# Finishing the down product of a decoder block tile by tile, with three steps held back instead of two

## The chip, the core and the metric

The kernel runs on one core of a Trainium2 chip. A core has a matrix engine (TensorE, "PE" in the profile, its weight loads "PEld"), a vector engine (VectorE, "DVE"), a scalar engine for activation functions (ScalarE, "ACT"), GpSimd ("POOL") and an engine that mostly issues transfers (SyncE, "SP"). Each engine works through its own queue of instructions in order and waits on semaphores that others raise. Sixteen DMA engines move data between the on-chip memory and DRAM; a transfer is started from the queue of SyncE or of ScalarE. The metric is the time of one execution on the device in microseconds (us), lower is better.

## The reference

The kernel computes one decoder block on 1024 tokens with 1024 channels in float32: a mixer (pooling and windowed attention, merged by gates, and an output projection), a residual with a norm, and then a feed-forward part, again with a residual and a norm. What the change touches are the norms and the last lines:

```python
def _rmsnorm(x, g):
    xf = x.astype(jnp.float32)
    r = lax.rsqrt(jnp.mean(xf * xf, axis=-1, keepdims=True) + EPS)
    return (xf * r * g.astype(jnp.float32)).astype(x.dtype)
...
    mix = jnp.einsum('bsd,de->bse', merged, w_out[l])
    x = x + _rmsnorm(mix, g_mix_post[l])

    h2 = _rmsnorm(x, g_mlp_pre[l])
    ff = jnp.einsum('bsf,fd->bsd',
                    jnp.square(jax.nn.relu(jnp.einsum('bsd,df->bsf', h2, w_up[l]))), w_down[l])
    x = x + _rmsnorm(ff, g_mlp_post[l])
```

So every token row of `ff` (1024 values) is squared and averaged, the root of that mean plus EPS is inverted, the row is scaled by it and by a gain, and the residual x1 is added.

## The kernel before, in words

**Precision and products.** Float32 matmuls are made of three passes: each operand is split into a high part and a low remainder (`split`, L97: a cast on ScalarE at L98 and a subtraction on VectorE at L99), and high x high, high x low and low x high are summed (`PASSES`, L32). The large products are done by a Strassen-like scheme: seven half-size products instead of eight, summed into the quarters of the result.

**The down product** (L945 to L1085) is the last stage. The token rows fall into 8 tiles of 128 (0 to 3 the upper half, 4 to 7 the lower), the channels into two halves of 512 (`dj` 0 and 1). The seven products run in the order `PRODUCTS = (1, 5, 2, 3, 6, 7, 4)`. Each has `NS = 8` steps over the 4096 hidden channels; a step is 24 matmuls (2 blocks x 4 tiles x 3 passes) into four banks of the accumulator memory, one a tile. The operands of a step are made two steps ahead (`AHEAD = 2`, `operands`, L975): a load of f (`raw`, four buffers), a weight block that is resident (24 buffers) or streamed, a difference of weights where the scheme wants one (L1004 for product 4), and two splits. The split parts of f have six buffers, so three steps' worth.

**Its end.** In product 4 the steps before the last `LATE = 2` go step by step over all four tiles; the last two are held back and then run tile by tile (L1078), so that tile 4 is complete first, then 5, 6 and 7. For each of them the bank is added to `u` (L1079, VectorE); `fin_half` squares it with a running sum on ScalarE (L1021) and multiplies by the gain in place on VectorE (L1022); then `finish` does the rest for tiles 4 and 5 together, then for 6, then for 7: add the two halves' sums (L1026), the reciprocal root in `rsqrt` (L101: root on ScalarE at L104, then small steps on VectorE at L106 to L116, a reciprocal with one Newton step), load x1 into a staging buffer (L1030), and for both halves one fused multiply and add and a store (L1033, L1034). The lower half's other channels (`v`) have had their square and gain after product 7 (L1073), and the upper half is finished after product 6 (L1084).

**The output projection** (L706 to L754) has the same norm in `mean_sq`: two squares with sums, an addition on VectorE (L710), `rsqrt`. `out_post` uses it on the projection, `out_norm` on the new residual rows, once each for 8 tiles. Transposes of the normed rows (L761) then feed the up product.

**Order.** A planner in the tile layer sets the order of the instructions on each engine out of the program and its own estimate of durations, allocates buffers and places the semaphores; the program's order is its priority. So the written order is not quite that on the engines.

Of the kernel before, what the change touches and what calls it, by code (L numbers as in the profile page):

```python
# [50 lines left out]
def block_kernel(ctx: ExitStack, tc, xt, x, consts, vecs, sinks, b_qkv, g_post, g_mlp, g_mlp_post,  # L51
                 w_qkv, w_u, w_g, w_pool, w_bp, w_ba, w_o, w_up, w_dn, x1_dram, spill, f_dram, out):
    nc = tc.nc
    act, dve, pool, pe = nc.scalar, nc.vector, nc.gpsimd, nc.tensor
# [27 lines left out]
    def at(tag, bufs, shape, dt=F32):  # L82
        return ap_.tile([P] + shape, dt, tag=tag, name=nm(tag), bufs=bufs)

    def bank(tag, shape=None):
        return ps.tile([P] + (shape or [512]), F32, tag=tag, name=nm(tag))

    def small(n=8, tag="sm"):
        return sp.tile([P, n], F32, tag=tag, name=nm(tag))

    def flat(t):
        return t.rearrange("p a b -> p (a b)")
# [8 lines left out]
    def rsqrt(out_r, sums, n):  # L101

        s = small()
        act.activation(s[:, :n], sums, AF.Sqrt, scale=1.0 / D, bias=eps)  # L104
        ms = small()
        dve.tensor_scalar(ms[:, :n], sums, 1.0 / D, EPS, ALU.mult, ALU.add)  # L106
        r = small()
        dve.reciprocal(r[:, :n], s[:, :n])
        t = small()
        if n == 1:  # L110
            dve.scalar_tensor_tensor(t[:, :1], r[:, :1], r[:, :1], ms[:, :1], ALU.mult, ALU.mult)
        else:
            dve.tensor_tensor(t[:, :n], r[:, :n], r[:, :n], ALU.mult)
            dve.tensor_tensor(t[:, :n], t[:, :n], ms[:, :n], ALU.mult)
        dve.tensor_scalar(t[:, :n], t[:, :n], -0.5, 1.5, ALU.mult, ALU.add)
        dve.tensor_tensor(out_r, r[:, :n], t[:, :n], ALU.mult)  # L116
# [83 lines left out]
    for n in range(NT):  # L200
        pe.matmul(bss[:, n:n + 1], sq[:, n * P:(n + 1) * P], ones, start=n == 0, stop=n == NT - 1)
    rsqrt(r1, bss[:, :NT], NT)


# [423 lines left out]
    for p in range(8):  # L628
# [4 lines left out]
        tag = "at" if p % 2 == 0 else "mm"  # L633
# [72 lines left out]
    def mean_sq(src_halves, junk_halves):  # L706
        a = small(2, "sq")
        for i in range(2):
            act.activation(junk_halves[i], src_halves[i], AF.Square, accum_out=a[:, i:i + 1])
        dve.tensor_tensor(a[:, 0:1], a[:, 0:1], a[:, 1:2], ALU.add)  # L710
        r = small(1, "rr")
        rsqrt(r, a[:, 0:1], 1)
        return r

    def halves(t):
# [148 lines left out]
    gfin_b = bcast(g_mlp_post, D)  # L864
# [54 lines left out]
    for p in range(1, NP):  # L919
# [3 lines left out]
        tag = "at" if p % 2 == 0 else "mm"  # L923
# [27 lines left out]
    rp = rpool.__enter__()  # L951
    dl = ctx.enter_context(tc.tile_pool(name="dl", bufs=16, reuse_waits="tile"))

    def acc4(name):
        return [dl.tile([P, 512], F32, tag="acc", name=nm(name), bufs=16) for _ in range(4)]
# [4 lines left out]
    sq = sp.tile([P, 2, NT], F32, tag="fsq", name="fsq", bufs=1)  # L960
    rr = sp.tile([P, NT], F32, tag="frr", name="frr", bufs=1)
    junk = dl.tile([P, 512], F32, tag="junk", name="junk", bufs=1)
    res = {}

    def resident(name, s_):
        t = rp.tile([P, 2, 512], F32, tag="w", name=nm(name))
# [8 lines left out]
    def operands(i, s_):  # L975

        if i == 1 and s_ in early_raw:
            ft, wt = early_raw[s_]
            resident("B11", s_)
        else:  # L980
            if i == 1:
                resident("B11", s_)
            ft = raw_tile()
            nc.sync.dma_start(ft, f_block(A_OF[i], s_))
            if i == 1:
                wt = res["B11", s_]
            elif i == 5:
                resident("B12", s_)
                wt = res["B11", s_]
                dve.tensor_tensor(wt, res["B12", s_], wt, ALU.subtract)  # L990
            elif i == 2:
                wt = streamed("B21", s_)
            elif i == 3:
                resident("B22", s_)
                wt = res["B22", s_]
            elif i == 6:
                wt = res["B11", s_]
                dve.tensor_tensor(wt, res["B22", s_], wt, ALU.subtract)
            elif i == 7:
                wt = res["B12", s_]  # L1000
                dve.tensor_tensor(wt, res["B22", s_], wt, ALU.subtract)
            else:
                wt = streamed("B21", s_)
                dve.tensor_tensor(wt, wt, res["B11", s_], ALU.subtract)  # L1004
        fo = wslot([2, 512]), wslot([2, 512])
        split(*fo, ft)
        wo_ = ar([2, 512]), ar([2, 512])
        split(*wo_, wt)
        opers[i, s_] = fo, wo_

    def down_mm(i, s_, bs, after, order):
        for s2, k2, t in order:
            fo, wo_ = opers[i, s2]
            for j, (fh, wh) in enumerate(PASSES):
                pe.matmul(bs[t], fo[fh][:, k2, t * P:(t + 1) * P], wo_[wh][:, k2, :],  # L1015
                          start=not after and s2 == 0 and k2 == 0 and j == 0,
                          stop=s2 == NS - 1 and k2 == 1 and j == 2, skip_group_check=after)

    def fin_half(n, dj, v):

        act.activation(junk, v, AF.Square, accum_out=sq[:, dj, n:n + 1])  # L1021
        dve.tensor_tensor(v, v, gfin_b[:, dj * 512:(dj + 1) * 512], ALU.mult)  # L1022

    def finish(n0, n1, hv):
        ns = slice(n0, n1)
        dve.tensor_tensor(sq[:, 0, ns], sq[:, 0, ns], sq[:, 1, ns], ALU.add)  # L1026
        rsqrt(rr[:, ns], sq[:, 0, ns], n1 - n0)
        for n in range(n0, n1):
            xs = stage([D])
            nc.sync.dma_start(xs, x1_dram[n])  # L1030
            for dj in range(2):
                o = xs[:, dj * 512:(dj + 1) * 512]
                dve.scalar_tensor_tensor(o, hv[dj][n % 4], rr[:, n:n + 1], o, ALU.mult, ALU.add)  # L1033
                nc.sync.dma_start(out[n][:, dj * 512:(dj + 1) * 512], o)  # L1034

    PRODUCTS = (1, 5, 2, 3, 6, 7, 4)
    LATE = 2
    steps = [(i, s_) for i in PRODUCTS for s_ in range(NS)]
    u, v, c11, c12 = acc4("u"), acc4("v"), acc4("c11"), acc4("c12")
    banks = {}  # L1040
# [4 lines left out]
    for j, (i, s_) in enumerate(steps):  # L1045
        if j + AHEAD < len(steps):
            operands(*steps[j + AHEAD])
        if s_ == 0 and i not in (2, 3):
            tag = "mm" if i in (5, 7) else "at"
            banks[i] = [bank(tag) for _ in range(4)]  # L1050
        bs = banks[{2: 1, 3: 5}.get(i, i)]
        if i != 4 or s_ < NS - LATE:
            down_mm(i, s_, bs, i in (2, 3), [(s_, k2, t) for k2 in range(2) for t in range(4)])
            if s_ < NS - 1:
                continue
        elif s_ < NS - 1:
            continue
        for t in range(4):
            if i == 1:
                act.copy(u[t], bs[t])  # L1060
            elif i == 5:
                act.copy(v[t], bs[t])
            elif i == 2:
                act.copy(c11[t], bs[t])
                fin_half(t, 0, c11[t])
            elif i == 3:
                act.copy(c12[t], bs[t])
            elif i == 6:
                dve.tensor_tensor(u[t], u[t], bs[t], ALU.add)
                dve.tensor_tensor(c12[t], c12[t], u[t], ALU.add)  # L1070
                dve.tensor_tensor(v[t], v[t], u[t], ALU.add)
                fin_half(t, 1, c12[t])
            elif i == 7:  # L1073
                dve.tensor_tensor(v[t], v[t], bs[t], ALU.add)
                dve.tensor_tensor(u[t], u[t], bs[t], ALU.add)
                fin_half(4 + t, 1, v[t])
            else:
                down_mm(i, s_, bs, False, [(s2, k2, t) for s2 in range(NS - LATE, NS) for k2 in range(2)])  # L1078
                dve.tensor_tensor(u[t], u[t], bs[t], ALU.add)  # L1079
                fin_half(4 + t, 0, u[t])  # L1080
                for n0, n1 in ((), ((4, 6),), ((6, 7),), ((7, 8),))[t]:
                    finish(n0, n1, (u, v))
        if i == 6:
            finish(0, 4, (c11, c12))  # L1084
    rpool.__exit__(None, None, None)  # L1085


# [68 lines left out]
```

## Time and profile before

| | us |
|---|---|
| median of 3 runs | 1163.75 (1163.31 to 1164.55) |
| the profiled execution | 1163.43 |
| its span, first to last instruction | 1161.6 |
| TensorE busy | 1137.1 |
| VectorE busy | 827.4 |
| ScalarE busy | 533.8 |
| granted TensorE clock | 0.996 |

In rows in order of time the columns are the start and the duration in us, the engine, the line of the program, the operation, the tile written and the tile read with their shapes, the count, and in brackets how long the engine had been idle before and what ended that. The chain of work is followed back from the last instruction to what released each one. Rows of waits give the engine that waited, what it waited for, the total in us, the number of times and the longest. Buffer numbers are left out of names: `at` and `mm` are accumulator banks, `u`, `v`, `c` sums of products, `fsq` the sums of squares, `sm` small tiles, `frr` the factors, `raw` loaded blocks, `wh` and `ar` their split parts.

### The profile page before, as it was taken

The page shows a single profiled execution, that of the slowest core. Times are in us where ns is not written, and L with a number is a line of the kernel's source. Part 1 is how long each engine was busy: PE and PEld are TensorE (multiplying, and loading weights), DVE is VectorE, ACT ScalarE, POOL GpSimd, SP SyncE. Part 2 cuts the span into 40 slices and gives each one's busy share as a digit, 9 for nine tenths or more (in the row PEclk, how much of TensorE's full clock was granted, in tenths as well). Part 3 has the DMA queues.
Part 4 walks back from the last instruction along what each step waited for, and adds up shares of the span by engine and source line. Part 5 has one row for each costly group of instructions (what it writes and reads, how often), then busy time and mean ns, then how long its engine had stood idle before and what let it go on. Part 6 is the DMA issues. An engine that isn't in the chain of part 4 may idle for free.

```text
span 1161.6 us, 14370 instructions
## 1 busy us (share of the span) xinstructions
PE 1137.1 (98%) x5356; PEld 941.3 (81%) x5356; DVE 827.4 (71%) x1337; ACT 533.8 (46%) x926; POOL 53.5 (5%) x66
## 2 busy tenths in 40 slices
PE   7999999999999999999999999999999999999995
PEld 6888888788888887888788888888888888888884
DVE  7767899888754585777998766667558945447795
ACT  6445655653332233464655453535344345344341
POOL 3411100000000050000000000000000000000000
PEclk9999999999999999999999999999999999999998
DMA  7202114545245453333266434353788564332852
GB/s 257 66 1 91 38 55 163 200 172 172 110 174 189 145 199 109 127 128 127 91 217 217 171 128 181 118 181 118 285 294 295 202 194 133 91 104 77 273 181 91
DMA packets 66167, 179.11 MB, mean 154 GB/s; under 512 B 6192, under 2 KB 6192, under 8 KB 66096
## 3 DMA queue, kind: packets, MB, share of 16 engines
q1 hardware_dynamic: 60480, 157.99, 40.3%
q10 hardware_dynamic: 5616, 20.19, 4.5%
q8 instruction: 42, 0.69, 0.3%
q14 instruction: 29, 0.24, 0.1%
HBM read 127.82 MB, written 50.33 MB: 153 GB/s over the span
## 4 chain that ended last, share of the span: by engine, by line
PE 91%; DVE 4%; ACT 2%; DMA 2%; issue 1%; SPq 0%; DVEq 0%; ACTq 0%
PE mm L408 21%; PE at L408 16%; PE at L1015 15%; PE mm L1015 11%; PE mm L345 8%; PE mm L732 5%; PE mm L347 4%; PE mm L147 3%; PE at L307 2%; PE at L268 2%; PE mm L153 1%; PE at L147 1%; PE at L300 1%; DMA st<-in_w_up_dram 1%; DVE T L99 1%
## 5 line engine op out<-in xcount | busy, mean ns | idle before, releaser
L1015 PE MATMUL at<-ar,wh 128*128 128x512 f32 x744 | 169.3, 389 | 0.0
L1015 PEld LDWEIGHTS at<-ar,wh 128*128 128x128 f32 x744 | 139.6, 188 | 29.0
L1015 PE MATMUL mm<-ar,wh 128*128 128x512 f32 x576 | 131.0, 389 | 0.0
L99 DVE TENSOR_TENSOR wh<-raw,wh 128x1024 fp32r<-128x1024 f32 x53 | 64.8, 1224 | 86.4 <-ACT wh L98 86.4
L1015 PEld LDWEIGHTS mm<-ar,wh 128*128 128x128 f32 x576 | 108.1, 188 | 22.5
L98 ACT CAST wh<-st 128x512 fp32r<-128x512 f32 (+1 forms) x106 | 67.0, 641 | 119.6 <-PE mm L408 36.9
L98 ACT CAST wh<-raw 128x1024 fp32r<-128x1024 f32 x53 | 55.8, 1053 | 134.5 <-PE at L1015 63.4
L99 DVE TENSOR_TENSOR wh<-st,wh 128x512 fp32r<-128x512 f32 (+1 forms) x106 | 82.9, 790 | 18.3 <-ACT wh L98 16.1
L408 PE MATMUL mm<-gr,wh 128*128 128x512 f32 x300 | 72.4, 391 | 0.1
L408 PE MATMUL mm<-T,wx 128*128 128x512 f32 x288 | 67.6, 389 | 0.0
L408 PEld LDWEIGHTS mm<-gr,wh 128*128 128x128 f32 x300 | 56.0, 188 | 12.0 <-ACT g L797 0.5
L408 PEld LDWEIGHTS mm<-T,wx 128*128 128x128 f32 x288 | 54.1, 188 | 11.2
L408 PE MATMUL at<-T,wx 128*128 128x512 f32 x252 | 59.1, 389 | 0.0
L408 PEld LDWEIGHTS at<-T,wx 128*128 128x128 f32 x252 | 47.3, 188 | 9.8
L408 PE MATMUL mm<-x,wh 128*128 128x512 f32 x216 | 51.5, 390 | 0.9 <-ACT g L415 0.9
L99 DVE TENSOR_TENSOR ar<-B,ar 128x1024 fp32r<-128x1024 f32 x37 | 45.1, 1220 | 7.3 <-ACT ar L98 7.3
L408 PEld LDWEIGHTS mm<-x,wh 128*128 128x128 f32 x216 | 40.4, 188 | 10.1 <-ACT g L415 1.7
L408 PE MATMUL at<-gr,wh 128*128 128x512 f32 x183 | 44.6, 390 | 0.0
L290 ACT ACTIVATE s<-s,nmx 128x256 f32<-128x256 f32 (+1 forms) x64 | 31.3, 493 | 26.5 <-DVE nmx L275 26.4
L98 ACT CAST ar<-B 128x1024 fp32r<-128x1024 f32 x37 | 38.9, 1050 | 9.0 <-DMA B<-in_w_dn_dram 4.7
L408 PEld LDWEIGHTS at<-gr,wh 128*128 128x128 f32 x183 | 34.3, 188 | 7.6 <-DVE wh L99 0.4
L650 DVE TENSOR_TENSOR g<-g,mm 128x512 f32<-128x512 f32 x32 | 20.6, 683 | 27.7 <-PE mm L347 27.6
(332 smaller groups left out, 2292.8 us busy)
## 6 DMA issues: line engine op xcount, KB each, us to landing
raw<-f_dram SPq DMA_DIRECT2D x53, 512.0 KB, 3.7
f_dram<-g SPq DMA_DIRECT2D x30, 512.0 KB, 3.3
B<-in_w_dn_dram SPq DMA_DIRECT2D x24, 512.0 KB, 6.3
st<-in_w_up_dram SPq DMA_DIRECT2D x22, 512.0 KB, 3.7
f_dram<-g ACTq DMA_DIRECT2D x17, 512.0 KB, 2.6
st<-in_w_g_dram SPq DMA_DIRECT2D x16, 512.0 KB, 3.7
g<-spill_dram SPq DMA_DIRECT2D x16, 512.0 KB, 4.4
raw<-in_w_dn_dram SPq DMA_DIRECT2D x16, 512.0 KB, 4.6
```

The source lines that it names most:

```text
L98: act.copy(hi, src)
L99: eng.tensor_tensor(lo, src, f32(hi), ALU.subtract)
L147: pe.matmul(bq, xs_[k][n // 4][:, xh, n % 4 * P:(n % 4 + 1) * P], wq[k][:, h, :], start=k == 0 and j == 0, stop=k == NK - 1 and j == 2)
L268: pe.matmul(sb[kv][:, i, :nk], qt[r, qx, m * P:(m + 1) * P], kx[r, k0:k0 + nk], start=j == 0, stop=j == 2)
L290: act.activation(s4[:, j, :nk], s4[:, j, :nk], AF.Exp, scale=-1.0, bias=nmx[:, h:h + 1], accum_out=den[:, h:h + 1])
L307: pe.matmul(yb.rearrange("p m q -> p (m q)"), vs[k0 // P + kb][:, vh, kv * HD:kv * HD + P], pts[kv][:, ph, kb, :], start=j == 0, stop=j == ...
L345: pe.matmul(bs[th], whi[:, k, :], rhs(k, hl, th), start=k == 0 and hl == 0, stop=False)
L347: pe.matmul(bs[th], wlo[:, k, :], rhs(k, 0, th), start=False, stop=k == nk - 1)
L408: pe.matmul(b, w[:, wh, kt, :], xo[kt][:, xh, :], start=not after and kt == 0 and j == 0, stop=kt == 3 and j == 2, skip_group_check=after)
L650: dve.tensor_tensor(z[:, sl], z[:, sl], bs[th], ALU.mult)
L732: pe.matmul(obs[n][dj], l, wos[k][whl][:, dj * 512:(dj + 1) * 512], start=k == 0 and hl == 0 and whl == 0, stop=k == NK - 1 and hl == 1)
L1015: pe.matmul(bs[t], fo[fh][:, k2, t * P:(t + 1) * P], wo_[wh][:, k2, :], start=not after and s2 == 0 and k2 == 0 and j == 0, stop=s2 == NS ...
```

## The change

It has four parts.

- `LATE` goes from 2 to 3: the last three steps of product 4 run tile by tile.
- Each of the tiles 4 to 7 is finished alone, directly behind its own square. A new `rsqrt_sum` takes the two halves' sums separately: for one column the root adds the second as its bias on ScalarE, with no addition on VectorE ahead of it. The squares are scaled by 1/32 so that the sums are means, and EPS is added to the sum that is known early, at once for all four tiles of a half (`add_eps`). The gain's result goes to `c11`, whose earlier contents are done with, and not back into `u`.
- x1 of tiles 4 to 7 is loaded ahead into the resident weights' buffers (`load_x1`), no longer into staging buffers at the end. The half `dj` 1 is put out first, and the first of tile 7's two stores goes by ScalarE's queue.
- `mean_sq` of the output projection uses `rsqrt_sum` as well.

```diff
+    ROOT_D = D ** -0.5
+
+    def rsqrt_sum(out_r, a, b, n=1):
+        s = small()
+        ms = small()
+        if n == 1:
+            act.activation(s[:, :1], a, AF.Sqrt, bias=b)
+            dve.tensor_tensor(ms[:, :1], a, b, ALU.add)
+        else:
+            dve.tensor_tensor(ms[:, :n], a, b, ALU.add)
+            act.activation(s[:, :n], ms[:, :n], AF.Sqrt)
         r = small()
         dve.reciprocal(r[:, :n], s[:, :n])
...
     def mean_sq(src_halves, junk_halves):
         a = small(2, "sq")
         for i in range(2):
-            act.activation(junk_halves[i], src_halves[i], AF.Square, accum_out=a[:, i:i + 1])
-        dve.tensor_tensor(a[:, 0:1], a[:, 0:1], a[:, 1:2], ALU.add)
+            act.activation(junk_halves[i], src_halves[i], AF.Square, scale=ROOT_D, accum_out=a[:, i:i + 1])
+        b = small()[:, :1]
+        dve.tensor_scalar(b, a[:, 0:1], EPS, None, ALU.add)
         r = small(1, "rr")
-        rsqrt(r, a[:, 0:1], 1)
+        rsqrt_sum(r, a[:, 1:2], b)
         return r
...
-    def finish(n0, n1, hv):
-        ns = slice(n0, n1)
-        dve.tensor_tensor(sq[:, 0, ns], sq[:, 0, ns], sq[:, 1, ns], ALU.add)
-        rsqrt(rr[:, ns], sq[:, 0, ns], n1 - n0)
-        for n in range(n0, n1):
-            xs = stage([D])
-            nc.sync.dma_start(xs, x1_dram[n])
-            for dj in range(2):
-                o = xs[:, dj * 512:(dj + 1) * 512]
-                dve.scalar_tensor_tensor(o, hv[dj][n % 4], rr[:, n:n + 1], o, ALU.mult, ALU.add)
-                nc.sync.dma_start(out[n][:, dj * 512:(dj + 1) * 512], o)
+    def load_x1(n):
+        t = rp.tile([P, 2, 512], F32, tag="w", name=nm("xf"))
+        nc.sync.dma_start(flat(t), x1_dram[n])
+        xf[n] = t
+
+    def add_eps(ns, dj):
+        dve.tensor_scalar(sq[:, dj, ns], sq[:, dj, ns], EPS, None, ALU.add)
+
+    def fin_out(n, hv):
+        if n not in xf:
+            t = stage([2, 512])
+            nc.sync.dma_start(flat(t), x1_dram[n])
+            xf[n] = t
+        for dj in (1, 0):
+            o = xf[n][:, dj, :]
+            dve.scalar_tensor_tensor(o, hv[dj][n % 4], rr[:, n:n + 1], o, ALU.mult, ALU.add)
+            (nc.scalar if dj and n == NT - 1 else nc.sync).dma_start(out[n][:, dj * 512:(dj + 1) * 512], o)
...
-    LATE = 2
+    LATE = 3
...
             else:
+                n = 4 + t
                 down_mm(i, s_, bs, False, [(s2, k2, t) for s2 in range(NS - LATE, NS) for k2 in range(2)])
                 dve.tensor_tensor(u[t], u[t], bs[t], ALU.add)
-                fin_half(4 + t, 0, u[t])
-                for n0, n1 in ((), ((4, 6),), ((6, 7),), ((7, 8),))[t]:
-                    finish(n0, n1, (u, v))
+                fin_sq(n, 0, u[t])
+                fin_gain(0, c11[t], u[t])
+                rsqrt_sum(rr[:, n:n + 1], sq[:, 0, n:n + 1], sq[:, 1, n:n + 1])
+                fin_out(n, (c11, v))
+        if i == 7:
+            add_eps(slice(4, NT), 1)
+            for n in range(4, NT):
+                load_x1(n)
         if i == 6:
-            finish(0, 4, (c11, c12))
+            add_eps(slice(0, 4), 1)
+            rsqrt_sum(rr[:, 0:4], sq[:, 0, 0:4], sq[:, 1, 0:4], 4)
+            for n in range(4):
+                fin_out(n, (c11, c12))
```

More of the change, by code (lines that the diff above doesn't have):

```diff
@@ L106, in rsqrt @@
         dve.tensor_scalar(ms[:, :n], sums, 1.0 / D, EPS, ALU.mult, ALU.add)
+        r = small()
+        dve.reciprocal(r[:, :n], s[:, :n])
+        t = small()
+        if n == 1:
+            dve.scalar_tensor_tensor(t[:, :1], r[:, :1], r[:, :1], ms[:, :1], ALU.mult, ALU.mult)
+        else:
+            dve.tensor_tensor(t[:, :n], r[:, :n], r[:, :n], ALU.mult)
+            dve.tensor_tensor(t[:, :n], t[:, :n], ms[:, :n], ALU.mult)
+        dve.tensor_scalar(t[:, :n], t[:, :n], -0.5, 1.5, ALU.mult, ALU.add)
+        dve.tensor_tensor(out_r, r[:, :n], t[:, :n], ALU.mult)
+    ROOT_D = D ** -0.5
+    def rsqrt_sum(out_r, a, b, n=1):
+        s = small()
+        ms = small()
+        if n == 1:
+            act.activation(s[:, :1], a, AF.Sqrt, bias=b)
+            dve.tensor_tensor(ms[:, :1], a, b, ALU.add)
+        else:
+            dve.tensor_tensor(ms[:, :n], a, b, ALU.add)
+            act.activation(s[:, :n], ms[:, :n], AF.Sqrt)
         r = small()
@@ L962, in block_kernel @@
     junk = dl.tile([P, 512], F32, tag="junk", name="junk", bufs=1)
-    res = {}
+    res, xf = {}, {}
     def resident(name, s_):
@@ L1017, in down_mm, with fin_sq, fin_gain @@
                           stop=s2 == NS - 1 and k2 == 1 and j == 2, skip_group_check=after)
+    def fin_sq(n, dj, v):
+        act.activation(junk, v, AF.Square, scale=ROOT_D, accum_out=sq[:, dj, n:n + 1])
+    def fin_gain(dj, o, v):
+        dve.tensor_tensor(o, v, gfin_b[:, dj * 512:(dj + 1) * 512], ALU.mult)
     def fin_half(n, dj, v):
-        act.activation(junk, v, AF.Square, accum_out=sq[:, dj, n:n + 1])
-        dve.tensor_tensor(v, v, gfin_b[:, dj * 512:(dj + 1) * 512], ALU.mult)
-    def finish(n0, n1, hv):
-        ns = slice(n0, n1)
-        dve.tensor_tensor(sq[:, 0, ns], sq[:, 0, ns], sq[:, 1, ns], ALU.add)
-        rsqrt(rr[:, ns], sq[:, 0, ns], n1 - n0)
-        for n in range(n0, n1):
-            xs = stage([D])
-            nc.sync.dma_start(xs, x1_dram[n])
-            for dj in range(2):
-                o = xs[:, dj * 512:(dj + 1) * 512]
-                dve.scalar_tensor_tensor(o, hv[dj][n % 4], rr[:, n:n + 1], o, ALU.mult, ALU.add)
-                nc.sync.dma_start(out[n][:, dj * 512:(dj + 1) * 512], o)
+        fin_sq(n, dj, v)
+        fin_gain(dj, v, v)
+    def load_x1(n):
[13 more added lines that the diff above has]
+            (nc.scalar if dj and n == NT - 1 else nc.sync).dma_start(out[n][:, dj * 512:(dj + 1) * 512], o)
     PRODUCTS = (1, 5, 2, 3, 6, 7, 4)
-    LATE = 2
+    LATE = 3
     steps = [(i, s_) for i in PRODUCTS for s_ in range(NS)]
```

## The prediction

> **What bounds the kernel now.** I read the page's busy shares and chain first, to see whether anything but TensorE counts, then the stage table for what lies behind the last matmul, then that stretch in order of time.
>
> ```profile
> PE 1137.1 (98%) x5356; PEld 941.3 (81%) x5356; DVE 827.4 (71%) x1337; ACT 533.8 (46%) x926; POOL 53.5 (5%) x66
> PE 91%; DVE 4%; ACT 2%; DMA 2%; issue 1%; SPq 0%; DVEq 0%; ACTq 0%
> 1149.40:1161.60 12.20, 0.04 (x1) 0.00 (x0) 8.13 (x22) 1.31 (x4) 0.00 (x0) 0.62 0.59 216
> ```
>
> TensorE is busy for 98% of the span and carries 91% of the chain; a saving on another engine counts only where TensorE waits for it, or behind its last matmul. The third row (columns: PE, PEld, DVE, ACT, POOL busy) is that second place: of the last 12.20 us TensorE works 0.04, VectorE 8.13 in 22 instructions. The same stretch in order of time, with the last product's matmuls in the first row and the cadence of the product before it, from the chain, in the second:
>
> ```profile
> 1105.76 43.68 PE L1015 MATMUL at<-ar,wh 128*128 128x512 f32 x192
> 1062.40 43.52 PE mm L1015 x192
> 1141.32 0.69 DVE L1079 TENSOR_TENSOR u<-u,at 128x512 f32<-128x512 f32 x1 [4.90 <-PE at L1015]
> 1142.04 0.63 ACT L1021 ACTIVATE junk<-u 128x512 f32<-128x512 f32 x1 [7.06 <-DVE u L1079]
> 1142.58 0.18 ACT L1021 ACTIVATION_READ_ACCUMULATOR junk<-u 128x1 f32 x1
> 1144.04 0.69 DVE L1079 TENSOR_TENSOR u<-u,at 128x512 f32<-128x512 f32 x1 [0.55 <-PE at L1015]
> 1145.09 0.63 ACT L1021 ACTIVATE junk<-u 128x512 f32<-128x512 f32 x1 [2.33 <-DVE u L1079]
> 1147.32 0.68 DVE L1079 TENSOR_TENSOR u<-u,at 128x512 f32<-128x512 f32 x1
> 1151.83 0.68 DVE L1079 TENSOR_TENSOR u<-u,at 128x512 f32<-128x512 f32 x1
> 1153.98 0.75 DVE L1033 SCALAR_TENSOR_TENSOR st<-v,frr,st 128x512 f32<-128x512 f32 x1
> 1154.65 0.69 DVE L1022 TENSOR_TENSOR u<-u,bc 128x512 f32<-128x512 f32 x1
> 1155.25 0.15 DVE L1026 TENSOR_TENSOR fsq<-fsq 128x1 f32<-128x1 f32 x1
> 1155.44 0.29 ACT L104 ACTIVATE sm<-fsq,eps 128x1 f32<-128x1 f32 x1 [2.11 <-DVE fsq L1026]
> 1155.77 0.16 DVE L108 RECIPROCAL sm<-sm 128x1 f32<-128x1 f32 x1 [0.17 <-ACT sm L104]
> 1156.60 0.75 DVE L1033 SCALAR_TENSOR_TENSOR st<-u,frr,st 128x512 f32<-128x512 f32 x1
> 1157.27 0.74 DVE L1033 SCALAR_TENSOR_TENSOR st<-v,frr,st 128x512 f32<-128x512 f32 x1
> 1154.10 4.28 SPq L1034 DMA_DIRECT2D out_dram<-st  x4
> DMA to landing us min/median/max: 2.0/2.1/2.6
> ```
>
> Matmuls end at 1105.76 + 43.68 = 1149.44, one each 43.52 / 192 = 0.2267 us. The last 48 (two steps) run tile by tile, 12 a tile, so tiles 4 to 7 should be summed 36, 24, 12 and 0 matmuls before the end: 1141.28, 1144.00, 1146.72, 1149.44. The adds (L1079) start at 1141.32, 1144.04, 1147.32, 1151.83: 0.04 behind TensorE for two tiles, then 0.6 and 2.39 late, because VectorE is still on tiles 4 and 5, finished together, and tile 6. A tile gets 12 x 0.2267 = 2.72 us of TensorE time but needs about 4 of VectorE. Behind the last add stand square, gain, sum, root, reciprocal and two output steps, to 1157.27 + 0.74 = 1158.01. SyncE's last store is issued by 1158.38 and lands 2.1 later; the span ends at 1161.6, 3.59 behind the last VectorE instruction.
>
> **The change part by part.** *Three steps held back.* TensorE's work is the same 192 matmuls; the last 72 instead of 48 run by tile, 18 x 0.2267 = 4.08 us a tile. In the order of the changed program's instructions two matmuls of tile 5 stand within tile 4's eighteen, ahead of the first that reads step 7's low weights. Tile 4 is therefore complete 52 matmuls before the end, tiles 5 to 7 36, 18 and 0: 1137.65, 1141.28, 1145.36, 1149.44. The tile-ordered stretch now opens a step earlier, so step 7's operands are needed sooner:
>
> ```profile
> 1132.73 4.47 PE L1015 MATMUL at<-ar,wh 128*128 128x512 f32 x19
> 1131.22 1.23 DVE L1004 TENSOR_TENSOR raw<-raw,B 128x1024 f32<-128x1024 f32 x1 [0.24 <-DMA raw<-in_w_dn_dram]
> 1132.97 1.05 ACT L98 CAST wh<-raw 128x1024 fp32r<-128x1024 f32 x1 [3.44 <-PE at L1015]
> 1133.93 1.05 ACT L98 CAST ar<-raw 128x1024 fp32r<-128x1024 f32 x1
> 1134.06 1.22 DVE L99 TENSOR_TENSOR wh<-raw,wh 128x1024 fp32r<-128x1024 f32 x1 [1.62 <-ACT wh L98]
> 1135.20 1.22 DVE L99 TENSOR_TENSOR ar<-raw,ar 128x1024 fp32r<-128x1024 f32 x1
> ```
>
> They cannot come earlier: the cast at 1132.97 waits 3.44 us for the buffers of step 4, whose matmuls end there (first row). The low weights are done at 1135.20 + 1.22 = 1136.42, readable some 0.05 later (an add follows TensorE by 0.04). Their first reader is the 16th of the 72; the last matmul starts at 1149.44 - 0.39 = 1149.05, so it is due 56 x 0.2267 earlier, at 1136.36. TensorE would stall about 0.1 us; without the two matmuls in between it would be 0.55. Bounds 0 and 0.55; I take 0.1, and every later tile moves by it.
>
> *The finish of a tile.* Per tile VectorE has the add, the gain (into c11, so it need not wait for the square), the sum, reciprocal, three small steps down to the factor, and two output steps. From rows: square 0.72 after the add's start (1141.32 to 1142.04), its sum read 0.72 later (1142.58 + 0.18 = 1142.76), the root directly behind on ScalarE with a gap of 0.03 (as from root to reciprocal, 1155.73 to 1155.77) and 0.30 long, reciprocal 0.03 later: 1.80 behind the add. Reciprocal to first output step is 1156.60 - 1155.77 = 0.83, then 0.67 to the second and 0.67 until the next instruction (1153.98 to 1154.65). The next add can start 3.97 after the add. The gap of the root is unknown, since no root directly behind its own square was recorded: at the low end 0, at the high end 0.32, by which the square at 1145.09, which also waits for ScalarE's own earlier result, is later behind its add than that at 1142.04 (1.05 against 0.72). I take 0.03, because the other two short waits on a finished neighbour are of that size.
>
> *Summed.* Adds start at 1137.65 + 0.1 + 0.04 = 1137.79, then at the later of VectorE free and tile done: 1141.76 (done 1141.42), 1145.73 (1145.50), 1149.70 (1149.58). The last reciprocal comes at 1149.70 + 1.80 = 1151.50 instead of 1155.77: 4.27 us sooner. All behind it keeps its length: two output steps, then SyncE's issue and landing. The next-to-last store goes by ScalarE's queue, idle by then; the last is still SyncE's, and nothing of the end is gained by that. Ends: 4.5 (no stall, VectorE never late: reciprocal at 1149.48 + 1.77), and with 0.32 at each root 4.29 a tile, last add 1150.66, reciprocal at 1152.78, gain 2.99.
>
> *The x1 loads.* Four loads leave the end for buffers that free up in the fourth product, on SyncE's queue between blocks of f:
>
> ```profile
> 979.60 3.71 SPq L984 DMA_DIRECT2D raw<-f_dram  x2
> L984 SPq DMA_DIRECT2D raw<-f_dram x9: 359/359/360, 961.2 to 999.3; - x9
> 981.70 1.22 DVE L99 TENSOR_TENSOR wh<-raw,wh 128x1024 fp32r<-128x1024 f32 x1 [0.39 <-ACT wh L98]
> DMA to landing us min/median/max: 3.3/4.4/5.9
> ```
>
> The second f load of the first row issues at 979.60 + 3.71 - 0.36 = 982.95, as the split at 981.70 frees its buffer; with four such buffers it is cast four steps (21.8 us) on. A load of x1 lands in 5.9 at the worst (last row, L1030), and the one split that each x1 load waits for is the one just ahead of what the f block behind it waits for. Cost 0, covered by those four buffers; without them 4 x 0.36 us of issue. In the old place nothing is gained either, since the output steps there wait for reciprocals. Two additions of eps, some 0.15 each (L1026's row), lie beside matmuls of products six and seven.
>
> *The mean squares of the output projection (L706).* All 16 lose the hop from ScalarE to VectorE and back; the instruction count stays.
>
> ```profile
> PE at L408 <- DVE f_first L440: 1.1, 1, 1.1
>   DVE sq L710: 3.3, 11
> 539.72 0.62 ACT L98 CAST wh<-st 128x512 fp32r<-128x512 f32 x1 [1.61 <-PE mm L408]
> 540.25 0.63 ACT L709 ACTIVATE st<-x 128x512 f32<-128x512 f32 x1
> 541.95 0.29 ACT L104 ACTIVATE sm<-sq,eps 128x1 f32<-128x1 f32 x1
> 543.71 1.28 DVE L753 SCALAR_TENSOR_TENSOR x<-x,rr,bc 128x1024 f32<-128x1024 f32 x1
> 544.97 1.03 PE L761 MATMUL at<-cst,x 128*128 128x128 f32 x8
> ```
>
> ScalarE waited 3.3 us in all for these additions, but of TensorE's waits from 470 to 600 only the first row's 1.1 us lies behind VectorE, in a stretch it fills with other work. So I put it at 0: TensorE's matmuls cover it. Bounds: a gain of 1.1, and on the other side what the new order at tile 7 can do (below).
>
> **Rivals.** *VectorE's count sets the end.* The old stretch has 35 VectorE instructions from 1141.32 to 1158.01, 16.69 us; the new one 36. If the stretch keeps that length and only starts 3.53 earlier (1137.79), with one small step of 0.15 added, the gain is 3.4 and the time 1160.4. For it: VectorE is late on every tile but the first in my own sum. Against it: the old stretch holds waits (4.90 and 0.55 ahead of adds, 0.17 ahead of the reciprocal) that the order removes. The Trainium skill (VectorE: DVE Perf Modes, Rules for kernel authors) says of chained operations to minimize their count and not the semaphores; by it alone the saved hops would be worth nothing and this rival would hold. The rows from 1155.25 to 1155.77 speak against the rule here: the hop to the root costs 0.52 with one VectorE instruction of 0.15 in it.
>
> *The root's own wait.* 0.32 for each tile: gain 2.99, 1160.8, still faster.
>
> *The projection gives it back.* In the changed order ScalarE makes a cast of up weights between tile 7's second square and its root; that cast waits for TensorE to free a buffer. If it waits, tile 7's normed rows (543.71 + 1.28 = 544.99) come later, the transposes at 544.97 stall, and VectorE, which has no gap from there to f_first, passes it on one for one. From 4.3 us late on the gain is gone; at 6.6 the kernel is slower by 2.3, at 1166.1. Against it: the buffer is free at 539.72, before the squares start at 540.25, so I expect the cast to wait for nothing and the rows to be some 0.5 us earlier.
>
> *Step 7 late.* The subtraction at 1131.22 already waits 0.24 for its load. The cast that needs it starts at 1133.93, 1.48 behind the subtraction's end; what the load is later beyond that stalls TensorE as long. At 2 us beyond it the gain is 2.3 and the time about 1161.5. Against it: nothing is added to SyncE's queue in that product.
>
> **How the numbers follow.** The sum stands against the profiled execution, 1163.43 us (span 1161.6), 0.32 under the median of the three runs, 1163.75. Median less 4.27 is 1159.5. Chances: the sum, gain 3.7 to 4.6, 0.66; VectorE's count 0.10; the root's own wait 0.09; step 7 late or other losses up to the gain 0.10; the projection so late that it is slower 0.05. The low end is 4.5 off the median with 0.5 for the spread of runs, 1158.7; the high end the root's wait, 1160.8, and the same 0.5: 1161.3. About 0.2%, 2.3 us, is what a measurement can tell from none: faster 0.85 (the first three), same 0.10, slower 0.05.
>
> **What would show it.** Right: adds of the last product near 1137.8, 1141.8, 1145.7, 1149.7; each root within 0.1 of its square's sum; last output step near 1153.0; TensorE's end moved by under 0.3; no new wait of TensorE at L756 or L785, the projection's matmuls and transposes. Wrong: a gap of 0.3 ahead of each root, VectorE's lateness growing from tile to tile past 0.5, or TensorE waiting in the last 72 matmuls or around the transposes.

## The result, and the profile after

The changed kernel took 1159.95 us in the median of its runs (1159.07 to 1161.53), the kernel before 1163.76 us beside it; the ratio is 0.9967 with an interval of 0.9957 to 0.9978. That is 3.8 us faster, 0.33% (2.6 to 5.0 us by the interval), against a forecast of 4.27.

The execution that was profiled took 1161.12 us with a span of 1159.3, which is more than the median, so times counted from its start must not be compared with the earlier profile without care. The first view below is the busy time by stretch of the run: the kernel before first, then the changed one (start and end, length, busy times of PE, PEld, DVE, ACT and POOL with their counts, granted clock, DMA share, GB/s). Then come the matmuls of the last product and the whole end in order of time, of the changed kernel.

```profile
40.00:60.00 20.00, 18.27 (x129) 15.64 (x128) 14.84 (x50) 10.07 (x32) 7.83 (x18) 1.00 0.08 27
```

```profile
40.00:60.00 20.00, 18.02 (x119) 15.26 (x118) 13.70 (x47) 9.68 (x30) 6.67 (x16) 0.91 0.08 28
```

```profile
1107.37 43.97 PE L1039 MATMUL at<-ar,wh 128*128 128x512 f32 x192
1135.68 1.22 DVE L99 TENSOR_TENSOR wh<-raw,wh 128x1024 fp32r<-128x1024 f32 x1 [1.90 <-ACT wh L98]
1136.82 1.22 DVE L99 TENSOR_TENSOR ar<-raw,ar 128x1024 fp32r<-128x1024 f32 x1
1138.09 12.83 PEld L1039 LDWEIGHTS at<-ar,wh 128*128 128x128 f32 x57 [0.38 <-DVE ar L99]
1139.58 0.69 DVE L1116 TENSOR_TENSOR u<-u,at 128x512 f32<-128x512 f32 x1 [1.54 <-PE at L1039]
1143.56 0.68 DVE L1116 TENSOR_TENSOR u<-u,at 128x512 f32<-128x512 f32 x1
1147.53 0.68 DVE L1116 TENSOR_TENSOR u<-u,at 128x512 f32<-128x512 f32 x1
1151.50 0.68 DVE L1116 TENSOR_TENSOR u<-u,at 128x512 f32<-128x512 f32 x1
1152.22 0.63 ACT L1045 ACTIVATE junk<-u 128x512 f32<-128x512 f32 x1 [2.92 <-DVE u L1116]
1152.22 0.69 DVE L1048 TENSOR_TENSOR c<-u,bc 128x512 f32<-128x512 f32 x1
1152.76 0.19 ACT L1045 ACTIVATION_READ_ACCUMULATOR junk<-u 128x1 f32 x1
1152.97 0.16 DVE L126 TENSOR_TENSOR sm<-fsq 128x1 f32<-128x1 f32 x1
1152.97 0.29 ACT L125 ACTIVATE sm<-fsq 128x1 f32<-128x1 f32 x1
1153.30 0.16 DVE L131 RECIPROCAL sm<-sm 128x1 f32<-128x1 f32 x1 [0.17 <-ACT sm L125]
1154.14 0.75 DVE L1069 SCALAR_TENSOR_TENSOR xf<-v,frr,xf 128x512 f32<-128x512 f32 x1
1154.81 0.74 DVE L1069 SCALAR_TENSOR_TENSOR xf<-c,frr,xf 128x512 f32<-128x512 f32 x1
1154.92 0.37 ACTq L1070 DMA_DIRECT2D out_dram<-xf  x1
```

What to see. Between 40 and 60 us the granted clock was 0.91 in this execution and 1.00 in the earlier one, and TensorE began 10 matmuls fewer there (119 against 129); in the thirteen profiled executions of this record the last product begins at 1106.79 to 1107.97 in the four with 0.91 there and at 1104.97 to 1106.40 in the nine with 1.00. That stretch is far from anything that was edited, so times are counted from here on from the start of the last product. Its first matmul started at 1107.37 against 1105.76, 1.61 later, and the span still ended 2.3 earlier. From that first matmul to the end of the span it is 1159.3 - 1107.37 = 51.93 us, before 1161.6 - 1105.76 = 55.84: the end gained 3.91. The median before less 3.91 is 1159.85, so the median of the change (1159.95) is accounted for by the end alone.

Within the end, the four adds stand 3.98, 3.97 and 3.97 apart, where they stood 2.72, 3.28 and 4.51 apart before. The root starts 0.02 behind the reading of its sum (1152.76 + 0.19 = 1152.95), beside VectorE's own addition of the same two numbers, and the reciprocal 1.80 behind the add. The last VectorE instruction ends at 1155.55, 4.21 behind the last matmul (1107.37 + 43.97 = 1151.34); before, it was 1158.01 - 1149.44 = 8.57.

### The profile page after: what moved, and what is told of

The parts are those of the page before. It is cut to its first block, busy times and chain, and to the rows that moved or that the text cites. A ratio compares the mean times of both kernels' runs of the same rounds, so it can differ in the third digit from the quotient of the medians.

```text
span 1159.3 us, 14412 instructions
## 1 busy us (share of the span) xinstructions
PE 1138.6 (98%) x5356; PEld 942.0 (81%) x5356; DVE 828.6 (71%) x1339; ACT 534.6 (46%) x927; POOL 53.7 (5%) x66
## 4 chain that ended last, share of the span: by engine, by line
PE 88%; DVE 5%; ACT 3%; DMA 2%; issue 2%; SPq 0%; DVEq 0%; ACTq 0%
PE mm L431 21%; PE at L431 16%; PE at L1039 14%; PE mm L1039 11%; PE mm L368 7%; PE mm L756 5%; PE mm L370 4%; PE mm L170 2%; PE at L330 2%; PE at L291 2%; PE at L323 1%; PE mm L176 1%; DMA st<-in_w_up_dram 1%; DVE T L99 1%; ACT s L211 1%
```

## The experiments

The theory was that the end is a chain on VectorE of 3.97 us a tile, set by its waits as well as by its instructions, laid against 4.08 us of matmuls a tile. The main rival was that the number of VectorE instructions alone sets the end; the smaller ones were that the projection or the loads of x1 carry some of the difference. The measure is the distance from the first matmul of the last product to the end of the span, since it leaves the early part out. Four executions of the changed kernel, or of it with the x1 edit that moved nothing, give 51.93, 51.93, 51.91 and 51.82; the kernel before and the one with the projection alone give 55.84 and 55.60. So this measure leaves a tenth or two open, a quarter at the most. The quarter is one instruction: ScalarE's square of tile 5 starts 1.05 us behind its add in the kernel before and 0.79 behind it in the other execution (1143.78 to 1144.57); why, the runs do not show.

**Tile by tile, with two steps held back.** The changed kernel with

```diff
-    LATE = 3
+    LATE = 2
```

> All of the change, but the last two steps held back again instead of three. Theory (each tile's VectorE chain of some 3.5 to 4 us against TensorE's time for a tile): a tile takes TensorE 2.72 us, so VectorE falls behind from the second tile on, and its last instruction ends some 6.7 us behind the last matmul (4.2 with three steps, 8.6 before the change); gain against before 1.3 to 2.2 us, ratio about 0.9985. Rival (the number of VectorE instructions sets the end, and the change only lets them start 3.5 us sooner): without the earlier start no gain at all, 8.6 us behind the last matmul, ratio 1.000.

1161.04 us, ratio 0.9976 (0.9965 to 0.9987). The last product and its adds:

```profile
1104.97 43.68 PE L1039 MATMUL at<-ar,wh 128*128 128x512 f32 x192
1140.53 0.69 DVE L1116 TENSOR_TENSOR u<-u,at 128x512 f32<-128x512 f32 x1 [4.90 <-PE at L1039]
1144.50 0.68 DVE L1116 TENSOR_TENSOR u<-u,at 128x512 f32<-128x512 f32 x1
1146.05 0.68 DVE L1116 TENSOR_TENSOR u<-u,at 128x512 f32<-128x512 f32 x1
1149.49 0.67 DVE L1116 TENSOR_TENSOR u<-u,at 128x512 f32<-128x512 f32 x1
1154.08 0.74 DVE L1069 SCALAR_TENSOR_TENSOR xf<-c,frr,xf 128x512 f32<-128x512 f32 x1
```

VectorE idles 4.90 us ahead of the first add, because tile 4 is complete later, and from then on it has no time to make that up. Its last instruction ends at 1154.82, 6.17 behind the last matmul (1148.65), and the span's end (1158.6) is 53.63 behind the first one: 1.7 us more than with three steps. The gain, 55.84 - 53.63 = 2.2, is as expected, and the rival's 8.6 did not come. VectorE's end was 0.5 sooner than the theory's 6.7, since the order that the planner found puts the adds of tiles 6 and 7 between the small steps of the tile before, so that ScalarE squares them while VectorE finishes that tile; four chains laid strictly one behind another overstate the end once VectorE is the bound.

**Three steps held back, with the old finish.** The kernel before with

```diff
-    LATE = 2
+    LATE = 3
```

> The kernel before with three steps held back and nothing else: tiles 4 and 5 still finished together, the gain behind the square. Theory: the pair waits for tile 5, so the start 3.5 us sooner of tile 4 is worth 2.7 at most; the last VectorE instruction ends some 6.5 us behind the last matmul, gain 2.0 to 2.7 us, ratio about 0.998. Rival (count sets the end): the whole 3.4 us of the change's own gain comes from here, 5.1 us behind the last matmul.

1162.04 us, ratio 0.9986 (0.9972 to 1.0). The span (1160.6) ends 54.46 behind the first matmul of the product (1106.14): 1.4 less than before, 2.5 more than with the whole change. The rows:

```profile
1136.86 12.81 PEld L1015 LDWEIGHTS at<-ar,wh 128*128 128x128 f32 x57 [0.38 <-DVE ar L99]
1141.98 0.69 DVE L1079 TENSOR_TENSOR u<-u,at 128x512 f32<-128x512 f32 x1 [1.48 <-PE at L1015]
1148.64 0.68 DVE L1079 TENSOR_TENSOR u<-u,at 128x512 f32<-128x512 f32 x1
1150.11 0.69 DVE L1022 TENSOR_TENSOR u<-u,bc 128x512 f32<-128x512 f32 x1 [0.79 <-ACT junk L1021]
1154.72 0.16 DVE L108 RECIPROCAL sm<-sm 128x1 f32<-128x1 f32 x1 [0.17 <-ACT sm L104]
```

The product ends at 1106.14 + 43.95 = 1150.09, so tile 6 is complete 4.08 earlier, at 1146.01; its add comes at 1148.64, 2.6 late, because tiles 4 and 5 are finished together ahead of it. Held back without the finish of its own, the extra step mostly makes VectorE wait (1.48 ahead of the second add) for work that it then has to do in a heap. The gain is below the 2.0 to 2.7 us that were expected, and VectorE ends 6.89 behind the last matmul instead of 6.5. Tile 5's add came 2.44 sooner (35.84 behind the product's first matmul, before 38.28), but from it to VectorE's end it took 15.00 us, before 13.97: the planner now put tile 6's add behind the pair's four output steps, where it had stood between the small steps, so VectorE waits 0.79 for tile 6's square, a wait that the kernel before does not have. The rival, 5.1, is further off still. Each half of the change thus gives 1.4 and 2.2 us alone, and the two 3.9 together.

**The gain put back into its source.** The changed kernel with

```diff
-                fin_gain(0, c11[t], u[t])
+                fin_gain(0, u[t], u[t])
...
-                fin_out(n, (c11, v))
+                fin_out(n, (u, v))
```

> All of the change, but the gain is written back into u and so waits for the square. Same instructions on every engine, one wait more a tile. Theory: the reciprocal comes 0.39 us later behind each add (2.19 instead of 1.80), a tile takes 4.36 us instead of 3.97, more than TensorE's 4.08, so the lateness adds up: last add 1.2 us later, end 1.6 us later, gain 2.3 us, VectorE done 5.8 us behind the last matmul. Rival (count): nothing changes, 4.2 us.

1160.38 us, ratio 0.9968 (0.9957 to 0.998), which the runs do not tell from the change. The profile does. The first row is VectorE's count in the page of this kernel and the second that of the changed kernel; the others are the last product and the end of this one:

```profile
PE 1136.6 (98%) x5356; PEld 940.6 (81%) x5356; DVE 827.7 (71%) x1339; ACT 534.1 (46%) x927; POOL 53.5 (5%) x66
```

```profile
PE 1138.6 (98%) x5356; PEld 942.0 (81%) x5356; DVE 828.6 (71%) x1339; ACT 534.6 (46%) x927; POOL 53.7 (5%) x66
```

```profile
1105.27 43.94 PE L1039 MATMUL at<-ar,wh 128*128 128x512 f32 x192
1146.08 0.68 DVE L1116 TENSOR_TENSOR u<-u,at 128x512 f32<-128x512 f32 x1
1150.38 0.68 DVE L1116 TENSOR_TENSOR u<-u,at 128x512 f32<-128x512 f32 x1
1151.85 0.69 DVE L1048 TENSOR_TENSOR u<-u,bc 128x512 f32<-128x512 f32 x1 [0.79 <-ACT junk L1045]
1152.53 0.16 DVE L131 RECIPROCAL sm<-sm 128x1 f32<-128x1 f32 x1
1154.03 0.74 DVE L1069 SCALAR_TENSOR_TENSOR xf<-u,frr,xf 128x512 f32<-128x512 f32 x1
```

With the same 1339 instructions the adds stand 4.31 apart instead of 3.97, for the gain now waits 0.79 us for the square that reads the same buffer and then lies between the sum and the reciprocal (2.15 behind the add, not 1.80). VectorE ends at 1154.77, 5.56 behind the last matmul (1149.21) instead of 4.21, and the span 53.33 behind the first, 1.4 more than in the change (expected were 5.8 and 1.6). The rival of the count says no difference; it falls.

**A hop to the root and back.** The changed kernel, where VectorE adds the two sums ahead of the root instead of beside it, with as many instructions (for the down product's single tiles alone):

```diff
-        if n == 1:
+        if n == 1 and not hop:
...
-                rsqrt_sum(rr[:, n:n + 1], sq[:, 0, n:n + 1], sq[:, 1, n:n + 1])
+                rsqrt_sum(rr[:, n:n + 1], sq[:, 0, n:n + 1], sq[:, 1, n:n + 1], hop=True)
```

> All of the change, but in the last product the two halves' sums are added on VectorE ahead of the root again (the sum is needed for the Newton step anyway, so the number of instructions stays; the root waits for it). Theory: 0.2 us more a tile, 4.17 instead of 3.97, over TensorE's 4.08; the end is 0.8 us later, VectorE done 5.0 us behind the last matmul, gain about 3.0 us. Rival (only the count matters): nothing changes, 4.2 us.

1161.15 us, ratio 0.997 (0.9959 to 0.9981). Three rows of its last tile but one and the add behind them:

```profile
1149.22 0.16 DVE L128 TENSOR_TENSOR sm<-fsq 128x1 f32<-128x1 f32 x1
1149.41 0.20 ACT L129 ACTIVATE sm<-sm 128x1 f32<-128x1 f32 x1 [0.23 <-DVE sm L128]
1149.65 0.16 DVE L131 RECIPROCAL sm<-sm 128x1 f32<-128x1 f32 x1 [0.27 <-ACT sm L129]
1151.82 0.68 DVE L1116 TENSOR_TENSOR u<-u,at 128x512 f32<-128x512 f32 x1
```

The adds stand 4.13 apart (4.07 the first time), 0.16 more than in the change, and VectorE ends 4.76 behind the last matmul, 0.55 later than there; the span ends 52.49 behind the first. The addition and the wait behind it are 0.16 + 0.03 = 0.19, but the root without a second operand takes 0.20 and not 0.29, and so the first tile's reciprocal comes only 0.09 later behind its add. In the other three tiles the square also starts 0.05 to 0.07 later behind its add than in the change, which makes it 0.15 to 0.16; why is open. The end is 0.55 later where 0.8 was expected, and not 0 as the rival has it. The Trainium skill (VectorE: DVE Perf Modes, Rules for kernel authors) says of chained operations to minimize their count and not the semaphores. In this chain, which runs from VectorE through ScalarE and back, this run and the one before speak against it: at one and the same count one wait more a tile moved the end by 0.55 and by 1.4 us.

**The projection's mean squares alone.** The kernel before with `rsqrt_sum` and the new `mean_sq`, and nothing else of the change.

> The kernel before with the new mean square in the output projection alone. Theory: TensorE's matmuls cover it, ratio 1.000 within 0.001, TensorE's waits between 440 and 600 us unchanged (0.2 to 0.5 for weights, 1.1 for the first f). Rival: the saved hops shorten the stretch that VectorE fills, up to 1.1 us sooner, ratio 0.999.

1163.74 us, ratio 0.9996 (0.9987 to 1.0005): nothing that the runs can tell. TensorE was busy for 157.65 of the 160 us from 440 to 600, before for 157.66, and its wait for the first f is 1.1 us as before.

**The x1 loads at the end again.** The changed kernel without

```diff
-            for n in range(4, NT):
-                load_x1(n)
```

> All of the change, but x1 of tiles 4 to 7 is loaded into the three staging buffers again, tile 7's behind tile 4's store. Theory: no cost, since tile 7's x1 lands over 3 us before its first output step; gain 3.8 us, VectorE done 4.2 us behind the last matmul. Rival: the load lies on the path of the last tile, up to some 2 us later.

1159.04 us, ratio 0.9956 (0.9942 to 0.9969); 51.82 us from the first matmul to the end of the span. The loads ahead are worth nothing; the old place is as good, and the rival's 2 us did not come.

**The changed kernel again**, beside the first four of these.

> The changed kernel once more, beside the others. Gain 3.8 us, ratio 0.9967; the last VectorE instruction ends 4.2 us behind the last matmul. If the 1.6 us by which its profiled execution had been later already at the output projection came from the granted clock of that execution and not from the change, the arrival at the projection's transposes moves with the clock from run to run.

1159.12 us, ratio 0.9954 (0.9941 to 0.9967), and 51.93 us again. The clock between 40 and 60 us was 0.91 in the profiled execution again, and the last product began at 1107.97. In the two kernels that differ from this one only in the x1 loads or in the last store, the clock there was 1.00 and the product began at 1105.38 and 1105.41. So the later arrival goes with the clock, as the expectation had it; with the very same kernel, no profile shows the other case.

**Both last stores on SyncE's queue.** The changed kernel with

```diff
-            (nc.scalar if dj and n == NT - 1 else nc.sync).dma_start(out[n][:, dj * 512:(dj + 1) * 512], o)
+            nc.sync.dma_start(out[n][:, dj * 512:(dj + 1) * 512], o)
```

> Both halves of the last output tile are stored through SyncE's queue, as before the change; all else is the changed kernel. In the changed kernel's profile the span ends 3.75 us behind the end of the last VectorE instruction, in the kernel before 3.59. If the ScalarE queue costs those 0.16 us, the distance is 3.55 to 3.63 here; if it is what the transfer itself takes from one execution to the next, it stays between 3.6 and 3.8. The distance of the last VectorE instruction from the last matmul stays 4.2 us in both cases.

One run, 1158.95 us. VectorE ends at 1153.54, 4.20 behind the last matmul. The end of the span to a hundredth is in the busy times from 1150 us on, here of the kernel before, the changed kernel, the one with the x1 loads at the end again, and this one:

```profile
1150.00:1161.63 11.63, 0.00 (x0) 0.00 (x0) 7.53 (x21) 1.31 (x4) 0.00 (x0) 0.60 0.62 226
1150.00:1159.32 9.32, 1.35 (x6) 0.77 (x5) 5.11 (x12) 1.02 (x3) 0.00 (x0) 0.70 0.31 113
1150.00:1157.17 7.17, 0.00 (x0) 0.00 (x0) 3.11 (x9) 1.02 (x3) 0.00 (x0) 0.82 0.37 135
1150.00:1157.17 7.17, 0.00 (x0) 0.00 (x0) 3.14 (x9) 1.02 (x3) 0.00 (x0) 0.82 0.37 136
```

The span ends 3.63 behind VectorE here, at the edge of what was expected of one theory and within the other's, so this execution alone doesn't decide. All of them together say more. With SyncE alone it is 3.60 to 3.63 in five executions; with ScalarE's queue in the last tile it is 3.76 to 3.79 in seven, and 3.66 in the eighth, the one with the x1 loads at the end. In the traces the difference has two parts. From its issue to its landing SyncE's last store takes 2.07 to 2.09 us in the five and 2.12 to 2.14 in all eight: some 0.04 that goes with the queue. From that landing to the end of the span it is 1.50 to 1.52 in the five and 1.61 to 1.62 in the seven, but 1.50 in the eighth, which stores through ScalarE's queue as well. So the other 0.11 comes only where both edits are in, the store on ScalarE's queue and x1 loaded ahead; why is open.

**One small step less for each tile.** The changed kernel, where the factor -1/2 of the Newton step is put into the gain once at the start, so that the last two small steps become one (`minus2` is set for the down product's calls alone):

```diff
+        if minus2:
+            dve.scalar_tensor_tensor(out_r, t[:, :n], -3.0, r[:, :n], ALU.add, ALU.mult)
+            return
         dve.tensor_scalar(t[:, :n], t[:, :n], -0.5, 1.5, ALU.mult, ALU.add)
         dve.tensor_tensor(out_r, r[:, :n], t[:, :n], ALU.mult)
...
     gfin_b = bcast(g_mlp_post, D)
+    dve.tensor_scalar(gfin_b, gfin_b, -0.5, None, ALU.mult)
```

> The change with one small VectorE instruction less a tile: the factor -1/2 of the Newton step is put into the gain once, ahead of time, and the last two small steps become one. Theory: a tile takes 3.78 us, VectorE is never late, the last add starts 0.04 behind TensorE instead of 0.16, and the end is 0.3 us sooner: VectorE done 3.9 us behind the last matmul, gain 4.1 us. Rival (count): four instructions less over the end, 0.8 us sooner.

1160.32 us, ratio 0.9965 (0.9951 to 0.9978). The end:

```profile
1138.59 0.69 DVE L1120 TENSOR_TENSOR u<-u,at 128x512 f32<-128x512 f32 x1 [1.52 <-PE at L1043]
1142.37 0.68 DVE L1120 TENSOR_TENSOR u<-u,at 128x512 f32<-128x512 f32 x1
1146.29 0.69 DVE L1120 TENSOR_TENSOR u<-u,at 128x512 f32<-128x512 f32 x1
1150.37 0.69 DVE L1120 TENSOR_TENSOR u<-u,at 128x512 f32<-128x512 f32 x1 [0.21 <-PE at L1043]
```

The first spacing is 3.78, a step of 0.19 less than 3.97; the last is 4.08, TensorE's own, and the bracket names TensorE. VectorE has caught up, and from here a shorter chain saves only what lies behind the last add. VectorE ends 3.91 behind the last matmul and the span 51.60 behind the first, 0.3 less than in the change, as expected; the rival of the count had 0.8.

**Both of these together**, beside the changed kernel on the same chip.

> The changed kernel with the shorter Newton step (four VectorE instructions less in the last product) and both last stores on SyncE's queue. By the chain of VectorE the last VectorE instruction ends 3.9 us behind the last matmul (4.2 in the changed kernel), and the span some 3.65 us behind that (3.75 there): 7.55 instead of 7.95 behind the last matmul, so the median should be 0.4 us under that of the changed kernel on the same chip. If the runs differ among themselves by more than that, the medians will not show it and the profile has to.

> The changed kernel itself, beside the run above: the last VectorE instruction 4.2 us behind the last matmul, the span's end 7.9 to 8.0 us behind it, the median between 1159.1 and 1160.5.

1159.22 us (1158.75 to 1164.52) with the two edits, 1159.79 (1158.55 to 1163.94) for the changed kernel; the ratios to the kernel before are 0.997 (0.9955 to 0.9985) and 0.9966 (0.9957 to 0.9975). From the first matmul to the end of the span it is 51.40 against 51.91. The profile shows some half microsecond where 0.4 was expected. The medians point the same way and the ratios the other, so it is not shown in the time.

## Why the prediction was right

**TensorE's end and step 7.** The 192 matmuls stay, but the stall was mis-sized. The sum had 0.1 us, between bounds of 0 and 0.55; the product took 43.97 instead of 43.68, and 43.93 to 43.95 in the other kernels with three steps held back, against 43.68 in those with two: 0.25 to 0.29. The time at which the low weights are done was right (1138.04 in the profile after, 30.67 behind the first matmul; forecast 1136.42, 30.66 behind). The step that failed is when they are needed: I counted to the matmul, and what waits for them is the weight load ahead of it. That load itself brings in 128x128 of f; the low weights are the 128x512 that its matmul streams. But the wait for them stands at the load, which starts at 1138.09, 0.05 behind the split, so that the load is not done beforehand.

```profile
L1039 PEld LDWEIGHTS at<-ar,wh 128*128 128x128 f32 x744 | 139.6, 188 | 29.4 <-DVE ar L99 0.4
```

A load takes 188 ns (mean of the group, changed kernel), and the split's lateness of 0.11 by the forecast (1136.47 against 1136.36) and 0.19 make 0.30, close to the 0.25 to 0.29 that came. This is worked out from the rows; no run moved the wait. The row names the split as what it waited for, 0.4 in all. No rival had it: "step 7 late" was about the load from DRAM, and that was on time.

**The chain of a tile.** Right in every term: reciprocal 1.80 behind the add, 3.97 from add to add. The gap ahead of the root was 0.02 where 0.03 was taken and 0.32 feared, so the rival of the root's own wait did not happen. The square that the 0.32 was taken from is no fixed size either: it is the one of tile 5, 0.79 and not 1.05 behind its add in the projection's run. The hop's worth is shown by its experiment, 0.16 a tile; that the gain went to another buffer is worth twice that, 0.34 a tile.

**Add by add.** Counted from the first matmul of the product, the adds were forecast at 32.03, 36.00, 39.97 and 43.94, and came at 32.21, 36.19, 40.16 and 44.13: 0.18 or 0.19 late throughout, which is the stall's 0.29 less the 0.1 that was in the sum. The tiles' completion 52, 36, 18 and 0 matmuls before the end fits this.

**What lies behind.** "All behind it keeps its length" failed by a little: from the reciprocal to the end of the span it was 1161.63 - 1155.77 = 5.86, and is 1159.32 - 1153.30 = 6.02. The next-to-last store on ScalarE's queue was put at nothing; together with the x1 loads ahead it costs some 0.15 us, and 0.04 without them. So 4.27 - 0.19 - 0.16 = 3.92, which is the gain of the end in this pair of executions (3.91 above, from spans to a tenth). Against the projection's run, 55.60, the end gained 3.7.

**The projection and x1.** Both were put at 0 and measured at 0: 0.9996 for the first alone, 0.1 us for the second, which is the 0.11 behind the last landing. The cast between tile 7's squares and its root waited for nothing, as expected of a buffer that is free in time. In the changed kernel the row has no bracket (the first row is the kernel before, the others the changed one):

```profile
538.63 1.22 DVE L745 TENSOR_TENSOR x<-x,st 128x1024 f32<-128x1024 f32 x1
540.09 1.22 DVE L769 TENSOR_TENSOR x<-x,st 128x1024 f32<-128x1024 f32 x1
542.59 0.61 ACT L98 CAST wh<-st 128x512 fp32r<-128x512 f32 x1
543.10 0.29 ACT L125 ACTIVATE sm<-sq,sm 128x1 f32<-128x1 f32 x1
544.78 1.28 DVE L777 SCALAR_TENSOR_TENSOR x<-x,rr,bc 128x1024 f32<-128x1024 f32 x1
```

From the residual's addition to the normed rows it is 4.69 us, and was 543.71 - 538.63 = 5.08: 0.4 sooner, where "some 0.5" was forecast, and of no use to anyone. Of TensorE's waits there, those for `wohi` ahead of the projection's matmuls are 0.5 us where they were 0.2, and 0.3 to 0.5 in other executions with the new mean squares.

**The rival of the count.** It forecast 1160.4 and the sum 1159.5; the median, 1159.95, lies midway, so the time alone did not rule it out, and that it fell within the forecast is no proof of the mechanism. The trace is: by the count the stretch from the first add to VectorE's end would have lasted 16.69 + 0.15 = 16.84 us, and with its 36 instructions it lasted 1155.55 - 1139.58 = 15.97. So are the two experiments at an equal count.

## What to carry to other kernels

Behind the last matmul, lay out the consumer's chain for one tile (here 3.97 us) against the time that TensorE spends on a tile, and hold back as many steps as make the second just the longer: with fewer the consumer is the bound, as the run with two steps shows; that more than three would only make it idle is argued, no run held back four. In such a chain a wait counts like an instruction: write to another buffer so that two readers of one tile need not follow each other, and let the other engine take a second operand rather than wait for an addition. When operands are needed sooner, count to the weight load and not to its matmul.

## What was not expected

- In four of the thirteen profiled executions the granted clock is 0.91 between 40 and 60 us of the run and in nine it is 1.00; 118 to 120 matmuls start in that stretch in the four and 127 to 131 in the nine. In single microseconds it is not a clock of 0.91: in the changed kernel's profile it is 0.67, 0.50, 0.50 and 0.62 from 44 to 48 us and 1.00 around that, some 3.4 us at half the clock, and so in the other three. That is 1.7 us of clock missing, and the last product begins 1.7 us later in the mean of the four, nearly half of what this change gains. So a comparison of two profiles had to start from a point behind it.

```profile
45.00:47.00 2.00, 2.00 (x6) 1.60 (x5) 1.86 (x7) 0.07 (x1) 0.00 (x0) 0.50 0.00 0
42.35 1.83 PE L224 MATMUL at<-vec,qkv 128*128 128x1 f32 x15 [0.24 <-DVE qkv L212]
```

  In all four TensorE had been idle for 0.12 to 0.24 us between 41 and 43 us, as in the second row; so it had in two of the nine, and in the other seven not. All three profiles of the unedited changed kernel are among the four, but kernels that differ from it only at the end are in both groups. An idle moment there goes with it, then, but does not decide it alone.
- With ScalarE's queue for one of the last two stores of 256 KB, SyncE's last one lands 0.04 us later behind its issue. With x1 loaded ahead as well, the span ends another 0.11 later behind that landing.
- With the same split waited for, TensorE's weight loads idled 0.38 us and its matmuls lost 0.25 to 0.29.
